# Layer norms with mean and reciprocal deviation in PSUM, and a last norm that works on two tiles an instruction

## The chip, the cores and the metric

One core of one Trainium2 chip runs the kernel. The metric is the device time of one execution in microseconds (us); of several runs the median counts. The profile is of one execution, and its times count from the first instruction.

## What is computed

The reference is a decoder trunk of two layers on 256 positions and 2048 features, in float32. Each layer has a mixer (RWKV-7 time mixing, then differential attention) and a gated MLP, and a layer norm behind each of the four:

```python
def layer_norm(x, g, b):
    xf = x.astype(jnp.float32)
    mu = xf.mean(-1, keepdims=True)
    var = jnp.square(xf - mu).mean(-1, keepdims=True)
    return ((xf - mu) * lax.rsqrt(var + LN_EPS) * g + b).astype(x.dtype)

for i in range(DEPTH):
    h = rwkv7_mix(...) if i % 2 == 0 else diff_attn_mix(...)
    x = layer_norm(ALPHA * x + h, ln_g[i, 0], ln_b[i, 0])
    x = layer_norm(ALPHA * x + conv_glu(x, ...), ln_g[i, 1], ln_b[i, 1])
```

## The kernel before

Features lie on the 128 partitions and positions along the free dimension, so the activations `X` are 16 tiles of 128 x 256. A planner decides where tiles lie, sets the waits and puts each engine's instructions in order from the data dependences and the order of the code; the order of an engine's queue in the profile need not be that of the code.

Nearly all of the time goes into products of weights with activations. A weight block arrives as float32 (`raw`), ScalarE rounds its high half (`hi`, L210), VectorE subtracts that to get the low half (`lo`, L213), and TensorE multiplies with both. Two column blocks of 128 make one `hi` and one `lo` of 128 x 256.

A norm has these steps. `ln_add` adds the mixer's product to `X` tile by tile; GpSimd keeps running sums of the tiles and of their squares (`ln_acc`, L370). `ln_stats` lets TensorE add the partitions up with a matrix of 1/2048 (L345): the mean lands in the first half of one PSUM bank (`lnst`), the mean square in the second. ScalarE squares the mean (L419) and copies it to SBUF as `ln_dm` (L420), VectorE makes the variance `ln_v` (L421), and `rsqrt` gives the reciprocal deviation `ln_rs`, in SBUF: logarithm and exponential on ScalarE (L319, L320), then one Newton step of three VectorE instructions (L321 to L323).

The norm is applied in two ways. Three norms are applied in the middle of the kernel while TensorE works ahead: `Ahead.run` multiplies the next six weight columns (L896 to L898) with activations that are scaled but not yet normed, takes `ln_stats` behind the fifth of thirty items, and lets `ln_apply` go on a tile at a time. There GpSimd subtracts the mean from each tile (L435), and the rest goes by the letter for the tile in `LEAD["r"]`: for twelve tiles VectorE multiplies by `ln_rs` (L444) and ScalarE applies scale and bias, both given as a column of 128 values (L445); for one tile VectorE does both (L452, L453); for three VectorE multiplies by scale and `ln_rs` in one instruction (L457). Then the tile is split into high and low halves (L191 on ScalarE, L192 on VectorE). The products made ahead are corrected in `total` (L304 to L307), which reads `ln_dm` and `ln_rs` too.

The last norm has nothing to run beside. `ln_finish` subtracts the mean (L472) on VectorE for the six tiles of `FIN_V` and on GpSimd for the other ten, multiplies by scale and `ln_rs` on VectorE (L480), adds the bias on ScalarE (L482), and SP stores two tiles at a time (L484).

Of the kernel before, what the change touches and what calls it, by code (L numbers as in the profile page):

```python
# [8 lines left out]
F32 = mybir.dt.float32  # L9
F32R = mybir.dt.float32r  # L10
AF = mybir.ActivationFunctionType
ALU = mybir.AluOpType
AX = mybir.AxisListType

P = 128
T = 256
D = 2048
KT = D // P
# [20 lines left out]
ORDER = [0, 1, 14, 2, 3, 4, 5, 6, 7, 15, 8, 9, 10, 11, 12, 13]  # L39
DBL = 64 * 16 + 16  # L40
LEAD = dict(q=9, p=(), e=1, a=1, s=4, n=0.301, d=8, h=0.1, r='ACAAAAAAAAAAABBB')
FIN_V = (0, 2, 5, 8, 11, 14)
FIN_S = range(2, KT + 1, 2)


def _param_layout():
# [79 lines left out]
class Trunk:  # L126
# [199 lines left out]
    def ln_begin(self, ahead=None, share=False):  # L326

        if self.ln_st is None:
            mk = lambda name, **k: self.ctx.enter_context(self.tc.tile_pool(name=name, bufs=1, side="right", **k))
            st = mk("lnst", space=bass.MemoryType.PSUM).tile([P, 2 * T], F32, name="lnst")  # L330
            self.ln_st = [st[:, :T], st[:, T:]]
            pool = mk("lnp")
            self.ln_dm, self.ln_rs, self.ln_c, self.ln_m2, self.ln_v = (
                pool.tile([P, T], F32, name=f"ln_{n}") for n in ("dm", "rs", "c", "m2", "v"))
            self.ln_sq = pool.tile([P, 4, T], F32, name="ln_sq")
            self.ln_acc = pool.tile([P, 2 * T], F32, name="ln_acc")
        self.ln_n, self.ln_open, self.ln_share, self.ln_first = 0, False, share, []
        self.ln_ahead, self.ln_last = ahead, []
        if ahead is not None:
            ahead.columns()  # L340
# [71 lines left out]
    def ln_stats(self):  # L412

        nc = self.nc
        sx, sq = self.ln_st
        self.ln_colsum((self.ln_acc[:, :T], self.ln_acc[:, T:]))
        for n, tiles in enumerate(self.ln_last):
            self.ln_colsum(tiles, n == len(self.ln_last) - 1)
        nc.scalar.activation(out=self.ln_m2, in_=sx, func=AF.Square)  # L419
        nc.scalar.copy(out=self.ln_dm, in_=sx)  # L420
        nc.vector.scalar_tensor_tensor(out=self.ln_v, in0=sq, scalar=LN_EPS, in1=self.ln_m2, op0=ALU.add,  # L421
                                       op1=ALU.subtract)
        self.rsqrt(self.ln_v, self.ln_rs, T, self.ln_m2)

    def ln_plain(self, i, h):
        self.ln_stats()
# [38 lines left out]

    def ln_finish(self, i, h, out):
        nc = self.nc
        at = 0

        def center(j):  # L470
            eng = nc.vector if j in FIN_V else nc.gpsimd
            eng.tensor_tensor(out=self.X[:, j, :], in0=self.X[:, j, :], in1=self.ln_dm, op=ALU.subtract)  # L472

        for j in range(-2, KT):
            if j < KT - 2:
                center(j + 2)
            if j < 0:
                continue
            x = self.X[:, j, :]
            nc.vector.scalar_tensor_tensor(out=x, in0=x, scalar=self.p(f"ln_g{i}{h}", j), in1=self.ln_rs, op0=ALU.mult,  # L480
                                           op1=ALU.mult)
            nc.scalar.activation(out=x, in_=x, func=AF.Identity, bias=self.p(f"ln_b{i}{h}", j))  # L482
            if j + 1 in FIN_S:
                nc.sync.dma_start(out=out[:, at:j + 1, :], in_=self.X[:, at:j + 1, :])  # L484
                at = j + 1

    def lead(self, feed, group, *args, ramp=0, ahead=4):

# [975 lines left out]
```

## Time and profile before

| | before |
|---|---|
| median of 3 runs | 2576.1 us (2573.64 to 2580.8) |
| the profiled execution | 2568.52 us |
| its span, first to last instruction | 2566.5 us |
| TensorE busy | 2468.5 us, 96% |
| VectorE busy | 2053.8 us, 80% |
| ScalarE busy | 1645.2 us, 64% |
| GpSimd busy | 390.7 us, 15% |
| mean granted TensorE clock | 0.981 |

PE is TensorE's matmul side and PEld its weight loads, DVE is VectorE, ACT is ScalarE, POOL is GpSimd and SP is SyncE, which issues the transfers. Durations of neighbours on one engine overlap a little, so the distance from start to start is what a queue costs. A granted clock of 1.00 is 2.4 GHz, one of 0.50 is 1.2 GHz.

### The profile page before, as it was taken

Reading aid. Unit: us, or ns where it says so; the run is one execution under the profiler, and the core shown is the slowest. Engines: PE = TensorE matmul, PEld = TensorE weight load, DVE = VectorE, ACT = ScalarE, POOL = GpSimd, SP = SyncE. Lnnn points to the kernel's source line nnn. Section 1 sums busy time; section 2 is a strip of 40 time slices with the busy share of each in tenths; the row PEclk is TensorE's granted clock in tenths of the full one; section 3 lists DMA queues with packets and bytes.
Section 4 is the critical chain, followed back from the end, with each engine's and each line's share of the span. In section 5 each row is a group of like instructions: output and inputs, shape, how many; then the busy total and the mean of one; then the engine's idle time right before and its main releaser. Section 6 shows DMA issues by size and latency. Waiting matters only on the chain.

```text
span 2566.5 us, 54810 instructions
## 1 busy us (share of the span) xinstructions
PE 2468.5 (96%) x17598; PEld 2171.5 (85%) x17598; DVE 2053.8 (80%) x5100; ACT 1645.2 (64%) x4318; POOL 390.7 (15%) x456
## 2 busy tenths in 40 slices
PE   7999989899899999999999999999999999999996
PEld 6888778767788888888889899998888888888886
DVE  8977888887897777777777877779997777777776
ACT  5765555644576666666566766666676666666664
POOL 4343344332400000000111200003300000000111
PEclk9999999999999999999999999999999999999998
DMA  6544334344466555556766555556465555566664
GB/s 191 175 129 116 102 104 108 99 121 124 125 187 192 190 190 190 190 189 184 225 190 183 156 171 171 171 167 196 145 199 188 188 188 188 188 186 185 189 190 127
DMA packets 285186, 429.63 MB, mean 167 GB/s; under 512 B 69081, under 2 KB 91617, under 8 KB 284897
## 3 DMA queue, kind: packets, MB, share of 16 engines
q1 hardware_dynamic: 284896, 426.14, 55.0%
q8 instruction: 137, 2.24, 0.4%
q14 instruction: 153, 1.25, 0.2%
HBM read 421.03 MB, written 6.57 MB: 167 GB/s over the span
## 4 chain that ended last, share of the span: by engine, by line
PE 74%; DVE 4%; ACT 1%; issue 1%; DMA 1%; POOL 0%; ACTq 0%; DVEq 0%; SPq 0%; POOLq 0%
PE psd L225 42%; PE psd L226 21%; PE psd L293 1%; PE psd L291 1%; PE psd L292 1%; DVE lo L213 1%; PE psd L897 1%; PE psd L896 1%; PE psd L898 1%; PE lnst L345 1%; PE psd L221 1%; PE psd L223 1%; PE psd L222 1%; DMA raw<-in_rw_o 0%; PE pss L656 0%
## 5 line engine op out<-in xcount | busy, mean ns | idle before, releaser
L210 ACT CAST hi<-raw 128x256 fp32r<-128x256 f32 (+1 forms) x3128 | 1231.1, 405 | 676.5 <-PE psd L225 461.2
L213 DVE TENSOR_TENSOR lo<-raw,hi 128x256 fp32r<-128x256 f32 (+1 forms) x2984 | 1287.5, 442 | 404.4 <-ACT hi L210 369.4
L225 PE MATMUL psd<-S,hi 128*128 128x512 f32 x3004 | 1056.7, 396 | 0.4 <-ACT hi L210 0.4
L226 PE MATMUL psd<-S,lo 128*128 128x256 f32 x3004 | 842.2, 280 | 4.4 <-DVE lo L213 3.8
L225 PEld LDWEIGHTS psd<-S,hi 128*128 128x128 f32 x3004 | 566.0, 188 | 132.5 <-ACT hi L210 1.2
L226 PEld LDWEIGHTS psd<-S,lo 128*128 128x128 f32 x3004 | 565.8, 188 | 5.9 <-DVE lo L213 4.5
L225 PE MATMUL psd<-hs,hi 128*128 128x512 f32 x1290 | 451.4, 394 | 0.1
L226 PE MATMUL psd<-hs,lo 128*128 128x256 f32 x1290 | 361.5, 280 | 0.0
L225 PEld LDWEIGHTS psd<-hs,hi 128*128 128x128 f32 x1290 | 241.8, 187 | 56.5 <-ACT hi L210 1.0
L226 PEld LDWEIGHTS psd<-hs,lo 128*128 128x128 f32 x1290 | 243.1, 188 | 0.4 <-DVE lo L213 0.3
L363 POOL COPY ln_acc<-X 128x256 f32<-128x256 f32 x4 | 2.1, 528 | 1230.9 <-DVE X L397 1230.9
L213 POOL TENSOR_TENSOR lo<-raw,hi 128x256 fp32r<-128x256 f32 x144 | 130.4, 913 | 301.2 <-ACT hi L210 244.1
L223 PE MATMUL psd<-S,lo 128*128 128x256 f32 x480 | 140.6, 293 | 13.8 <-DVE lo L213 8.4
L221 PE MATMUL psd<-S,hi 128*128 128x256 f32 x480 | 141.6, 295 | 0.9 <-ACT hi L210 0.5
L222 PE MATMUL psd<-S,hi 128*128 128x256 f32 x480 | 141.4, 295 | 0.0
L223 PEld LDWEIGHTS psd<-S,lo 128*128 128x128 f32 x480 | 92.8, 193 | 22.3 <-DVE lo L213 12.8
L225 PE MATMUL psd<-S1r,hi 128*128 128x512 f32 x276 | 109.9, 427 | 1.4 <-ACT o_rs L1049 0.7
L370 POOL TENSOR_TENSOR ln_acc<-ln_acc,X 128x256 f32<-128x256 f32 x49 | 40.9, 834 | 402.4 <-DVE X L409 389.1
L221 PEld LDWEIGHTS psd<-S,hi 128*128 128x128 f32 x480 | 92.5, 193 | 5.7 <-ACT hi L210 1.5
L222 PEld LDWEIGHTS psd<-S,hi 128*128 128x128 f32 x480 | 92.8, 193 | 2.9 <-issue 2.7
L221 PE MATMUL psd<-S1r,hi 128*128 128x256 f32 x284 | 87.2, 307 | 1.4 <-ACT S1r L191 0.9
L897 PE MATMUL psd<-S,lo 128*128 128x258 f32 x256 | 75.4, 295 | 10.1 <-DVE lo L213 10.1
(297 smaller groups left out, 3823.5 us busy)
## 6 DMA issues: line engine op xcount, KB each, us to landing
raw<-in_ff_up SPq DMA_DIRECT2D x676, 256.0 KB, 3.4
raw<-in_ff_down SPq DMA_DIRECT2D x320, 256.0 KB, 3.0
raw<-in_rkv SPq DMA_DIRECT2D x192, 256.0 KB, 3.5
raw<-in_da_qk SPq DMA_DIRECT2D x122, 256.0 KB, 3.4
raw<-in_da_v SPq DMA_DIRECT2D x64, 256.0 KB, 3.1
raw<-in_da_o SPq DMA_DIRECT2D x64, 256.0 KB, 3.5
raw<-in_rw_o SPq DMA_DIRECT2D x50, 256.0 KB, 3.5
raw<-in_ff_down SPq DMA_DIRECT2D x32, 192.0 KB, 2.7
```

The source lines that it names most:

```text
L210: nc.scalar.copy(out=hi[:, :s * P], in_=r)
L213: eng.tensor_tensor(out=lo[:, :s * P], in0=r, in1=hi[:, :s * P].bitcast(F32), op=ALU.subtract)
L221: nc.tensor.matmul(ps[:, :T], lhsT=hi, rhs=xs[:, :T], start=first, stop=False)
L222: nc.tensor.matmul(ps[:, :T], lhsT=hi, rhs=xs[:, T:], start=False, stop=False)
L223: nc.tensor.matmul(ps[:, :T], lhsT=lo, rhs=xs[:, :T], start=False, stop=last)
L225: nc.tensor.matmul(ps, lhsT=hi, rhs=xs, start=first, stop=False)
L226: nc.tensor.matmul(ps[:, T:], lhsT=lo, rhs=xs[:, :T], start=False, stop=last)
L291: nc.tensor.matmul(o, lhsT=xh, rhs=hi, start=k == 0 and b == 0, stop=False)
L292: nc.tensor.matmul(o, lhsT=xh, rhs=lo, start=False, stop=False)
L293: nc.tensor.matmul(o, lhsT=xl, rhs=hi, start=False, stop=k == KT - 1 and b == T // P - 1)
L370: nc.gpsimd.tensor_tensor(out=self.ln_acc[:, hs], in0=self.ln_acc[:, hs], in1=t, op=ALU.add)
L897: nc.tensor.matmul(ps[:, 2:4 + T], lhsT=lo[:, w], rhs=x[:, 2:4 + T], start=False, stop=False)
```

## The change

The two tiles `ln_mean` and `ln_rs` become names for the two halves of the PSUM bank `lnst`: the mean stays where TensorE wrote it, and the exponential writes the reciprocal deviation over the mean square. The SBUF tile `ln_rs` is gone; the copy `ln_dm` stays for GpSimd and for `total`. The three VectorE instructions of the Newton step are written anew, so that each has the deviation as an operand. `ln_apply` and `total` are not edited, but their `ln_rs` is now in PSUM.

`ln_finish` is new. Four pairs of tiles (those that start at 4, 6, 8 and 10) are centred on GpSimd, tile by tile, and four on VectorE, two tiles in one instruction of 512 columns whose second operand is the mean, given twice. Then VectorE multiplies two tiles at a time by `ln_rs`, ScalarE applies scale and bias together to each tile, and SP stores the pair.

```diff
-FIN_V = (0, 2, 5, 8, 11, 14)
-FIN_S = range(2, KT + 1, 2)
+FIN_P = (4, 6, 8, 10)
 ...
-            self.ln_dm, self.ln_rs, self.ln_c, self.ln_m2, self.ln_v = (
-                pool.tile([P, T], F32, name=f"ln_{n}") for n in ("dm", "rs", "c", "m2", "v"))
+            self.ln_dm, self.ln_c, self.ln_m2, self.ln_v = (
+                pool.tile([P, T], F32, name=f"ln_{n}") for n in ("dm", "c", "m2", "v"))
+
+            self.ln_mean, self.ln_rs = self.ln_st
 ...
-        self.rsqrt(self.ln_v, self.ln_rs, T, self.ln_m2)
+        l, rs = self.ln_m2, self.ln_rs
+        nc.scalar.activation(out=l, in_=self.ln_v, func=AF.Ln)
+        nc.scalar.activation(out=rs, in_=l, func=AF.Exp, scale=-0.5)
+        nc.vector.tensor_tensor(out=l, in0=self.ln_v, in1=rs, op=ALU.mult)
+        nc.vector.scalar_tensor_tensor(out=l, in0=l, scalar=-0.5, in1=rs, op0=ALU.mult, op1=ALU.mult)
+        nc.vector.scalar_tensor_tensor(out=rs, in0=l, scalar=1.5, in1=rs, op0=ALU.add, op1=ALU.mult)
 ...
     def ln_finish(self, i, h, out):
         nc = self.nc
-        at = 0
-
-        def center(j):
-            eng = nc.vector if j in FIN_V else nc.gpsimd
-            eng.tensor_tensor(out=self.X[:, j, :], in0=self.X[:, j, :], in1=self.ln_dm, op=ALU.subtract)
-
-        for j in range(-2, KT):
-            if j < KT - 2:
-                center(j + 2)
-            if j < 0:
-                continue
-            x = self.X[:, j, :]
-            nc.vector.scalar_tensor_tensor(out=x, in0=x, scalar=self.p(f"ln_g{i}{h}", j), in1=self.ln_rs, op0=ALU.mult,
-                                           op1=ALU.mult)
-            nc.scalar.activation(out=x, in_=x, func=AF.Identity, bias=self.p(f"ln_b{i}{h}", j))
-            if j + 1 in FIN_S:
-                nc.sync.dma_start(out=out[:, at:j + 1, :], in_=self.X[:, at:j + 1, :])
-                at = j + 1
+        wide = lambda t: t.unsqueeze(1).broadcast_to([P, 2, T])
+        for j in range(0, KT, 2):
+            xs = self.X[:, j:j + 2, :]
+            if j in FIN_P:
+                for k in range(2):
+                    nc.gpsimd.tensor_tensor(out=xs[:, k], in0=xs[:, k], in1=self.ln_dm, op=ALU.subtract)
+            else:
+                nc.vector.tensor_tensor(out=xs, in0=xs, in1=wide(self.ln_mean), op=ALU.subtract)
+        for j in range(0, KT, 2):
+            xs = self.X[:, j:j + 2, :]
+            nc.vector.tensor_tensor(out=xs, in0=xs, in1=wide(self.ln_rs), op=ALU.mult)
+            for k in range(2):
+                nc.scalar.activation(out=xs[:, k], in_=xs[:, k], func=AF.Identity, scale=self.p(f"ln_g{i}{h}", j + k),
+                                     bias=self.p(f"ln_b{i}{h}", j + k))
+            nc.sync.dma_start(out=out[:, j:j + 2, :], in_=xs)
```

## Rows read from the trace of the kernel before

**Rows 1.** The page: engines' totals, and the chain's shares by engine.

```profile
PE 2468.5 (96%) x17598; PEld 2171.5 (85%) x17598; DVE 2053.8 (80%) x5100; ACT 1645.2 (64%) x4318; POOL 390.7 (15%) x456
...
PE 74%; DVE 4%; ACT 1%; issue 1%; DMA 1%; POOL 0%; ACTq 0%; DVEq 0%; SPq 0%; POOLq 0%
```

**Rows 2.** Chain of waits in the tail: start, us, engine, tile and line.

```profile
2546.66 0.38 ACT ln_m L419
2547.05 0.27 ACT ln_dm L420
2547.34 0.42 DVE ln_v L421
...
2550.12 0.86 DVE ln_m L321
...
2555.29 0.87 DVE X L480
2556.19 6.10 ACT X L482 x15
```

**Rows 3.** Timeline of the tail: start, us, engine, line, operation; then idle before.

```profile
2547.39 8.48 POOL L472 TENSOR_TENSOR X<-X,ln_dm 128x256 f32<-128x256 f32 x10 [14.63 <-ACT ln_dm L420]
2547.68 2.44 DVE L472 TENSOR_TENSOR X<-X,ln_dm 128x256 f32<-128x256 f32 x3
...
2548.25 0.42 ACT L320 ACTIVATE ln_rs<-ln_m 128x256 f32<-128x256 f32 x1
...
2556.19 6.50 ACT L482 ACTIVATE X<-X,par 128x256 f32<-128x256 f32 x16 [7.52 <-DVE X L480]
```

**Rows 4.** Timeline of the first middle norm: GpSimd, VectorE and ScalarE.

```profile
692.12 13.74 POOL L435 TENSOR_TENSOR X<-X,ln_dm 128x256 f32<-128x256 f32 x16 [11.75 <-ACT ln_dm L420]
693.95 0.96 DVE L321 TENSOR_TENSOR ln_m<-ln_rs 128x256 f32<-128x256 f32 x1
694.97 0.41 ACT L210 CAST hi<-raw 128x256 fp32r<-128x256 f32 x1 [0.31 <-PE psd L898]
695.69 0.41 ACT L210 CAST hi<-raw 128x256 fp32r<-128x256 f32 x1 [0.31 <-PE psd L898]
...
699.24 0.95 DVE L444 TENSOR_TENSOR X<-X,ln_rs 128x256 f32<-128x256 f32 x1
700.22 0.60 ACT L445 ACTIVATE X<-X,par 128x256 f32<-128x256 f32 x1 [4.12 <-DVE X L444]
700.99 0.94 DVE L213 TENSOR_TENSOR lo<-raw,hi 128x256 fp32r<-128x256 f32 x1
...
703.46 0.94 DVE L213 TENSOR_TENSOR lo<-raw,hi 128x256 fp32r<-128x256 f32 x1
703.57 0.60 ACT L445 ACTIVATE X<-X,par 128x256 f32<-128x256 f32 x1 [0.16 <-DVE X L444]
704.08 0.39 ACT L210 CAST hi<-raw 128x256 fp32r<-128x256 f32 x1
...
706.07 0.41 DVE L213 TENSOR_TENSOR lo<-raw,hi 128x256 fp32r<-128x256 f32 x1
706.40 0.41 DVE L444 TENSOR_TENSOR X<-X,ln_rs 128x256 f32<-128x256 f32 x1
```

**Rows 5.** TensorE's waits, 699 to 712: us in total, times, longest.

```profile
PE psd L897 <- DVE lo L213: 3.7, 3, 1.5
```

**Rows 6.** Busy time by stretch: PE, PEld, DVE, ACT, POOL; clock, DMA share, GB/s.

```profile
703.00:705.00 2.00, 0.54 (x4) 0.54 (x5) 2.00 (x3) 1.84 (x6) 2.00 (x4) 1.00 0.39 125
...
707.00:709.00 2.00, 2.00 (x11) 2.00 (x11) 2.00 (x7) 2.00 (x6) 0.00 (x0) 0.50 0.27 85
```

**Rows 7.** Instructions of lines L403 and L409: count, ns minimum/median/maximum, first and last start.

```profile
L403 DVE SCALAR_TENSOR_TENSOR t<-X,ln_c x44: 411/955/970, 651.3 to 2531.2; 128x256 f32<-128x256 f32 x44
L409 DVE TENSOR_TENSOR X<-t,psd x56: 399/414/422, 656.1 to 2544.9; 128x256 f32<-128x256 f32 x56
```

**Rows 8.** Groups by form: busy us, mean ns, idle before.

```profile
L659 DVE SCALAR_TENSOR_TENSOR s<-pss,B 128x512 f32<-128x512 f32 x8 | 5.5, 688 | 0.0
```

## What was predicted

> **What bounds the kernel now.** I read the page's totals first. TensorE is busy 96% of the span, and three quarters of the chain that ended last is TensorE [rows 1]. So an edit on VectorE, ScalarE or GpSimd is worth something only where TensorE has finished or stands still. The change touches the four layer norms, and there are two such kinds of place.
>
> The first is the tail. The chain of waits in its last stretch [rows 2] leaves TensorE when the last column sum ends, at about 2546.6 us, and then runs through ScalarE and VectorE for 16 us: square and copy, the variance, six VectorE instructions that start 0.865 us apart (2550.12 to 2555.29), the first scaled tile, and sixteen bias activations. The last of these ends at 2562.69 (6.50 us from 2556.19, [rows 3]); what lies behind it (last store, landing, end at 2566.5) is 3.8 us.
>
> The second is the three middle norms, which run beside products. In the first of them the timeline [rows 4] shows GpSimd subtracting the mean from sixteen tiles for 13.74 us, 0.86 us each. For all that time VectorE's instructions take 0.95 us and start 0.87 us apart; when GpSimd is done they take 0.41 us and start 0.33 us apart (706.07, 706.40). One of VectorE's jobs here is the low half of each weight block ("lo"), and TensorE waits for it three times, 3.7 us together [rows 5]. In the table by stretches TensorE is busy 0.54 of 2 us at 703 to 705, and at 707 to 709 it is fully busy at a granted clock of 0.50, which is 1.2 GHz [rows 6]. The other two middle norms, near 1430 and near 1830 us, repeat this almost to the instruction, so the rows stand for one of three and what is found for one counts three times.
>
> **Why the operand's place matters.** Two rows from the same stretches, where GpSimd adds up the column sums, differ in one thing [rows 7]. L403 reads two SBUF tiles: median 955 ns, at best 411. L409 reads one SBUF and one PSUM tile: 414 ns, never above 422. So beside GpSimd a VectorE instruction with one operand in PSUM keeps its 0.41 us. The change gives just that to every instruction that uses the mean or the reciprocal deviation: the three steps of the reciprocal root (each now has the deviation as an operand), the scaling of every tile, and the last norm's centring.
>
> **The middle norms, step by step.** From 693.95 to 706 VectorE runs six such instructions under GpSimd's load: three root steps, and the scaling of tiles 0, 1 and 2. Each goes from 0.87 to about 0.34 us start to start, 3.2 us less. The lo blocks and the splits keep two SBUF operands and their 0.87 us while GpSimd runs. I let the queue run again with these lengths, in the same order. The lo block of 700.99 ends at 699.2; before, it ended at 701.93. The one of 703.46 ends at 701.2. The one of 706.07 starts at 702.9 and, now inside GpSimd's stretch, ends at 703.8 instead of 706.5. A lo block feeds TensorE for 0.72 us: the hi casts, released by TensorE, are that far apart (694.97, 695.69 in [rows 4]). ScalarE's queue stood behind the activation of tile 0 until 700.22 [rows 4]; it moves 2.1 us ahead with that tile, so the hi halves are there. Then TensorE finds the first two blocks in time and waits some 1.8 us for the third, which it starts at 703.85 instead of 706.53, 2.7 us earlier. The next two blocks come 0.4 us late each, because GpSimd still runs until about 705.3. That leaves 1.9 us; I take 1.8. What is late next is again a lo block, behind two splits of 0.87 us.
>
> After the stall TensorE ran at half clock from 706.5 to 709.9 and there did what takes 2 us at full clock, so 1.4 us were lost. Since some 2.6 us of standing still remain, I keep this loss in the forecast; if the clock stays up, a norm gives 3.3 us. Behind that TensorE is fully busy for tens of us, so what it gains carries to the end. Bounds for one norm: 0 (the waits are only moved) to 3.3 us. Three norms: 5.4 us, between 0 and 9.9.
>
> **The tail, step by step.** Up to the exponential, which ends at 2548.67 [rows 3], nothing changes. Before, VectorE filled its wait for it with three centrings (2547.68 on). Now the centrings read the mean from the PSUM bank into which the exponential writes. That different engines are kept apart in one bank shows in [rows 2]: the variance needs the square, which ended at 2547.04, but starts at 2547.34, when ScalarE's copy from the same bank has ended. So I put the centrings behind the exponential.
>
> The Trainium skill, "PSUM — Partial Sum Buffer", section "PSUM bank collisions raise a hardware error", says that two engines must never be in one bank and the same 32 partitions together, reads included, and that the compiler orders them. That speaks against this change. By the rule the tail is as summed below; without it two centrings would hide in front of the root, 1.2 us better. The trace agrees with the rule by the 0.30 us of the variance.
>
> From 2548.70 VectorE then has three root steps of 0.34 us (1.0), four centrings of two tiles, and the first scaling. A 512-column instruction that reads PSUM with a broadcast operand took 688 ns [rows 8]; less the 0.07 us by which neighbours overlap (0.41 against 0.34), that is 0.62 apart, so 2.5 us for the centrings and 0.69 for the scaling. All four stand ahead of the first scaling in the code, so I count all four: ScalarE starts at 2552.9. The order is the planner's; with pair 0 alone ahead it is 1.9 us better.
>
> Now the price of one activation with scale and bias. Bias alone: sixteen in 6.50 us of 0.50 each, so 0.40 start to start [rows 3]. With both as columns the activation takes 0.60 us, and the next starts 0.51 us behind it (703.57, 704.08 in [rows 4]). Sixteen cost 15 x 0.51 + 0.60 = 8.25 us where they cost 6.50. ScalarE so becomes the bound of the tail: VectorE's pairs come every 0.62 us and ScalarE needs 1.02 for one. It ends at 2561.1 instead of 2562.69: 1.6 us gained, though its first input comes 3.3 us earlier. GpSimd's eight centrings (0.73 to 0.90 us each) end by 2554.6 and the last of them is needed near 2557; they are covered by over 2 us. Eight stores were and are issued by SP, one for two tiles, the last behind the last activation: nothing.
>
> Not shown in the trace: ScalarE or VectorE writing such a tile into PSUM. For VectorE I bound it by 0.34 and 0.87 us per instruction (the two states of the same instruction in [rows 4]) and take the lower, as reads of PSUM show it. Two columns-fed activations in a row: between 0.40 and 0.60 start to start; I take 0.51, which is the same instruction before another one. So the tail lies between 4.5 us gained and nothing.
>
> **The sum.** 1.6 + 5.4 = 7.0 us. The profiled execution would go from 2568.5 to 2561.5. It was 7.6 us faster than the median of the runs; put on the median, 2576.1 - 7.0 = 2569.1 us.
>
> **Rivals.**
> Half clock goes too. If TensorE's shorter stalls leave the clock at 1.0, each norm gives 3.3 us: 1.6 + 9.9 = 11.5, so 2564.6. For it: two of the three waits vanish or nearly so. Against: 2.6 us of waiting remain of 3.7, most of them in one piece, and what followed 3.7 us may follow 2.6.
>
> The middle norms give nothing. The lo blocks still queue behind splits at 0.87 us, and GpSimd, ending only 0.5 us sooner, could keep TensorE's last wait where it is, or the planner could order VectorE's queue otherwise. Only the tail is left: 2574.5. For it: six short instructions among long ones; against: 3.2 us less work on a queue in which, by the rows, one instruction follows the other.
>
> Slower: the contention stays although one operand is in PSUM. Then the root steps cost 0.87 us and a two-tile centring 1.73 while GpSimd runs, until 2554.4. That holds three root steps and 1.8 centrings; 2.2 centrings and the scaling follow by 2556.5, and ScalarE ends 8.25 us later, at 2564.7: 2.0 us slower, with no gain in the middle, 2578.1. It decides at a first scaled pair later than 2554.4. Against it stand [rows 7].
>
> **How the numbers follow.** Forecast 0.50, with a range of its own from 2567 to 2572; clock stays up 0.25; middle gives nothing 0.18; contention stays 0.07. The range of 8 in 10 reaches to the second and third cases: 2563.5 to 2575.5. A measurement of this kernel tells 0.3%, 7.7 us, from no change. The forecast lies just inside it: I give a little under half of it (0.22) and all of the second case to faster, 0.47. Slower by as much needs the contention and lost order in the middle norms, 0.03; same is 0.50.
>
> **What would show it.** In the changed profile: the root steps and scalings near 0.41 us while GpSimd runs; TensorE's waits for lo about 2.6 instead of 3.7 us a norm; granted clock 0.5 behind each or not; in the tail, no centring before the exponential's end, ScalarE's first activation near 2552.9 less what was gained earlier, sixteen of them 0.51 apart. I am wrong if VectorE's order in the middle norms is another, or if those instructions still take 0.95 us.

## The result, and the profile after

Six runs of each kernel beside each other gave 2560.57 us after (2552.46 to 2566.5) against 2576.76 before (2571.47 to 2583.35), a ratio of 0.9934 with a 95% interval from 0.9910 to 0.9957. The forecast was 2569.1 with a range from 2563.5, so the kernel became faster by more than was forecast, and its time lies outside the range.

Where the time went is read from the start of each norm's square on ScalarE, which opens its statistics, because there the stages can be told apart. In microseconds:

| profiled execution | first square at | to the 2nd | to the 3rd | to the last | last square to span's end |
|---|---|---|---|---|---|
| before | 691.40 | 731.03 | 398.68 | 725.55 | 19.84 |
| after | 697.24 | 727.96 | 396.88 | 722.32 | 17.60 |
| gain | -5.8 | 3.1 | 1.8 | 3.2 | 2.2 |

Behind the first square 10.3 us are gained: 8.1 in the middle norms (forecast 5.4) and 2.2 in the tail (forecast 1.6). Ahead of it the changed kernel was 5.8 us later in this pair of profiles, although every engine runs the same instructions in the same order there. Over all the profiled executions of this study that first square stood between 687.5 and 703.5 us. So the medians contain a scatter of some microseconds that arises ahead of the changed instructions, and the distances between the squares are the better measure.

In the page's totals of after (busy us, share of the span, instructions), VectorE has 13 us less to do than in [rows 1], and the other engines are within a few us of what they were:

```profile
PE 2472.6 (97%) x17598; PEld 2172.2 (85%) x17598; DVE 2040.8 (80%) x5090; ACT 1645.8 (64%) x4318; POOL 388.1 (15%) x454
```

VectorE's and GpSimd's timeline in the first middle norm of after, which answers to [rows 4] (start, us, engine, line, operation):

```profile
697.92 0.42 DVE L422 SCALAR_TENSOR_TENSOR ln_v<-lnst,ln_m 128x256 f32<-128x256 f32 x1 [2.29 <-PE psd L901]
697.97 13.61 POOL L441 TENSOR_TENSOR X<-X,ln_dm 128x256 f32<-128x256 f32 x16 [12.26 <-ACT ln_dm L421]
...
699.79 0.41 DVE L427 TENSOR_TENSOR ln_m<-ln_v,lnst 128x256 f32<-128x256 f32 x1
700.13 0.63 DVE L212 TENSOR_TENSOR lo<-raw,hi 128x256 fp32r<-128x256 f32 x1
700.68 0.41 DVE L428 SCALAR_TENSOR_TENSOR ln_m<-ln_m,lnst 128x256 f32<-128x256 f32 x1
...
702.77 0.41 DVE L458 TENSOR_TENSOR X<-X,lnst 128x256 f32<-128x256 f32 x1
703.10 0.99 DVE L212 TENSOR_TENSOR lo<-raw,hi 128x256 fp32r<-128x256 f32 x1
704.01 0.82 DVE L459 TENSOR_SCALAR X<-X,par 128x256 f32<-128x256 f32 x1
704.75 0.96 DVE L212 TENSOR_TENSOR lo<-raw,hi 128x256 fp32r<-128x256 f32 x1
705.63 1.84 DVE L191 TENSOR_TENSOR S<-X,S 128x256 fp32r<-128x256 f32 x2
707.39 0.96 DVE L212 TENSOR_TENSOR lo<-raw,hi 128x256 fp32r<-128x256 f32 x1
708.28 0.41 DVE L450 TENSOR_TENSOR X<-X,lnst 128x256 f32<-128x256 f32 x1
```

Three things are to be seen. Every instruction with one operand in "lnst", the PSUM tile, takes 0.41 us while GpSimd is at work, as forecast. The lo block behind a root step costs 0.55 us start to start (700.13 to 700.68), where two operands in SBUF were counted at 0.87; but behind two such instructions in a row it costs 0.91 (703.10 to 704.01). And the scaling of tile 2, which stood at 702.59 in the kernel before, ahead of a lo block and both splits of tiles 0 and 1, now comes behind them (708.28).

TensorE's waits in the 13 us that answer to [rows 5], and the busy table (us of PE, PEld, DVE, ACT, POOL; granted clock, DMA share, GB/s) for the stretch of its longest wait, to set beside [rows 6]:

```profile
PE psd L900 <- DVE lo L212: 0.6, 2, 0.3
```

```profile
707.24:709.24 2.00, 1.67 (x14) 1.41 (x12) 2.00 (x5) 0.52 (x2) 2.00 (x3) 1.00 0.00 1
```

TensorE waits 0.6 us where it waited 3.7, its longest wait is 0.3 where it was 1.5, and the granted clock stays at 1.00 (2.4 GHz).

How much of this lasts is read from the same matmuls in both kernels. The busy table (columns as above) has the first 113 matmuls from the square on and the 118 behind them, first before, then after:

```profile
691.42:710.70 19.28, 15.54 (x113) 14.91 (x112) 18.43 (x31) 10.93 (x30) 13.74 (x16) 0.91 0.21 66
710.70:724.48 13.78, 13.78 (x118) 13.78 (x117) 13.07 (x39) 12.58 (x38) 0.64 (x1) 1.00 0.58 173
```

```profile
697.26:711.51 14.25, 13.92 (x113) 13.41 (x112) 13.41 (x23) 8.74 (x24) 13.54 (x16) 1.00 0.27 77
711.51:727.15 15.64, 15.18 (x118) 14.12 (x117) 14.86 (x44) 14.26 (x41) 0.06 (x1) 1.00 0.51 155
```

The first 113 take 5.0 us less than before, the next 118 take 1.9 us more. Of the 5.0 us that the change gains where GpSimd subtracts, 1.9 are given back behind it, while GpSimd has nothing to do (0.06 us) and VectorE is busy for 14.86 of 15.64 us.

The tail of after, by the timeline, beside [rows 2] and [rows 3]:

```profile
2544.40 0.38 ACT L420 ACTIVATE ln_m<-lnst 128x256 f32<-128x256 f32 x1 [0.80 <-PE lnst L346]
2545.12 5.52 POOL L479 TENSOR_TENSOR X<-X,ln_dm 128x256 f32<-128x256 f32 x8 [14.63 <-ACT ln_dm L421]
2545.98 0.39 ACT L426 ACTIVATE lnst<-ln_m 128x256 f32<-128x256 f32 x1
2546.40 0.42 DVE L427 TENSOR_TENSOR ln_m<-ln_v,lnst 128x256 f32<-128x256 f32 x1 [0.90 <-ACT lnst L426]
2546.86 0.42 DVE L428 SCALAR_TENSOR_TENSOR ln_m<-ln_m,lnst 128x256 f32<-128x256 f32 x1
2547.32 0.43 DVE L429 SCALAR_TENSOR_TENSOR lnst<-ln_m,lnst 128x256 f32<-128x256 f32 x1
2547.78 2.48 DVE L481 TENSOR_TENSOR X<-X,lnst 128x512 f32<-128x512 f32 x4
2550.18 4.86 DVE L484 TENSOR_TENSOR X<-X,lnst 128x512 f32<-128x512 f32 x8
2550.89 7.97 ACT L486 ACTIVATE X<-X,par 128x256 f32<-128x256 f32 x16 [4.52 <-DVE X L484]
```

VectorE stands idle until the exponential has ended, then does the root, all four centrings and only then the first scaling. ScalarE's sixteen activations follow at 0.49 us each and end at 2558.86, 14.46 us behind the square; before it was 16.03 (2546.66 to 2562.69).

### The profile page after: what moved, and what is told of

Read it like the earlier page. It is cut to its first block, busy times and chain, and to the rows that moved or that the text cites. A ratio compares the mean times of both kernels' runs of the same rounds, so it can differ in the third digit from the quotient of the medians.

```text
span 2562.0 us, 54782 instructions
## 1 busy us (share of the span) xinstructions
PE 2472.6 (97%) x17598; PEld 2172.2 (85%) x17598; DVE 2040.8 (80%) x5090; ACT 1645.8 (64%) x4318; POOL 388.1 (15%) x454
## 4 chain that ended last, share of the span: by engine, by line
PE 83%; DVE 10%; DMA 2%; issue 2%; ACT 2%; POOL 1%; SPq 0%; DVEq 0%; ACTq 0%; POOLq 0%
PE psd L224 42%; PE psd L225 22%; PE psd L220 3%; PE psd L222 3%; PE psd L221 3%; DVE lo L212 3%; PE psd L291 1%; PE psd L292 1%; PE psd L290 1%; DVE mx L776 1%; DVE S L191 1%; DMA raw<-in_rw_o 1%; PE pss L1145 1%; DVE S1r L191 1%; ACT hi L209 1%
## 5 line engine op out<-in xcount | busy, mean ns | idle before, releaser
L222 PE MATMUL psd<-S1r,lo 128*128 128x256 f32 x284 | 84.8, 299 | 1.5 <-DVE lo L212 1.4
```

Of the source, the lines that this page charges most:

```text
L222: nc.tensor.matmul(ps[:, :T], lhsT=lo, rhs=xs[:, :T], start=False, stop=last)
```

## The experiments

### Which place gives the time, and how sure it is

Four kernels were compared with the kernel before in one set of interleaved runs. Two are the kernels before and after, unchanged.

> The kernel before once more, to see how far one profile differs from another. Stages are measured by the start of the squaring of the mean (the first ScalarE instruction of a norm's statistics): 691.4, 1422.4, 1821.1 and 2546.7 us in the profile of before, 697.2, 1425.2, 1822.1 and 2544.4 in that of after. Theory A (the gain of the change lies only behind the first norm's statistics, about 10 us: 8.1 in the three distances between them, 2.2 in the tail; the rest of the measured 17 us is scatter of the first stage, whose queues are the same in both kernels): ratio 1.000, the three distances again 731.0, 398.7 and 725.6 within 1 us, the tail 19.8 from the last square to the end, and a first stage anywhere between 685 and 700. Theory B (the first stage too is shorter after the change, by some 7 us on the mean): the first stage within 2 us of 691.4 here, and in the kernels that carry the change some 7 us below.

> The changed kernel once more. Theory A (gain only behind the first statistics): ratio near 0.996 (10 us), distances 728.0, 396.9, 722.3 within 1 us, tail 17.6. Theory B (first stage too): ratio 0.9934 again, first stage below 688.

The third has the middle norms' part alone: the deviation in PSUM for every norm, and the last norm in its old form (from the kernel after):

```diff
-FIN_P = (4, 6, 8, 10)
+FIN_V = (0, 2, 5, 8, 11, 14)
...
-        wide = lambda t: t.unsqueeze(1).broadcast_to([P, 2, T])
...
+        def center(j):
+            eng = nc.vector if j in FIN_V else nc.gpsimd
+            eng.tensor_tensor(out=self.X[:, j, :], in0=self.X[:, j, :], in1=self.ln_dm, op=ALU.subtract)
...
+            nc.vector.scalar_tensor_tensor(out=x, in0=x, scalar=self.p(f"ln_g{i}{h}", j), in1=self.ln_rs, op0=ALU.mult,
+                                           op1=ALU.mult)
+            nc.scalar.activation(out=x, in_=x, func=AF.Identity, bias=self.p(f"ln_b{i}{h}", j))
```

> Mean and reciprocal deviation in PSUM as in the change, but the last norm written as before: single tiles, centred from the SBUF copy of the mean, scale and reciprocal deviation in one VectorE instruction, bias alone on ScalarE. Theory A: the three distances as after (728.0, 396.9, 722.3), gain 8 us there. In the tail, theory C (what counts there is that the root steps no longer wait for GpSimd): three root steps 0.35 instead of 0.87 us, so the first activation 1.6 us earlier than before and, with 0.40 us from one to the next, a tail of 18.2; ratio 0.996. Theory D (the pairs and the joint activation make the gain in the tail): tail 19.8 as before, ratio 0.997.

The fourth has the last norm's part alone: only there is the deviation in PSUM (from the kernel after):

```diff
-            self.ln_mean, self.ln_rs = self.ln_st
+            self.ln_mean, self.ln_rs = self.ln_st[0], self.ln_sb
...
+        if not wide:
+            return self.rsqrt(self.ln_v, self.ln_rs, T, self.ln_m2)
+        self.ln_rs = self.ln_st[1]
...
-                self.ln_stats()
+                self.ln_stats(True)
```

> The three middle norms as before, with the reciprocal deviation in SBUF; only the last norm has it in PSUM and is written as in the change. Theory A: distances 731.0, 398.7, 725.6 as before, tail 17.6, ratio 0.9991 (2.2 us). Theory B (first stage too, since the queues of that stage are those of the change): first stage some 7 us shorter, ratio 0.9965.

| kernel | median, us | ratio to before (95%) | distances of the squares | tail |
|---|---|---|---|---|
| before again | 2570.46 | 0.9999 (0.9986 to 1.0012) | 730.6, 398.9, 725.6 | 19.6 |
| after again | 2560.94 | 0.9966 (0.9953 to 0.9979) | 727.8, 397.0, 722.4 | 17.6 |
| middle norms alone | 2558.35 | 0.9963 (0.9949 to 0.9978) | 727.3, 396.8, 722.2 | 16.6 |
| last norm alone | 2568.79 | 0.9991 (0.9978 to 1.0004) | 730.6, 399.6, 725.7 | 17.6 |

The distances repeat to within 0.7 us in the first column and 0.2 in the last, and each part moves only its own columns. The middle column is less sure: a kernel below with the same middle norms has 398.2 there. The second comparison's ratio is worth 0.0034 x 2570.5 = 8.7 us, where the first's medians gave 16.2; the 10.3 us of the stages lie between. As a ratio they are 0.9960, inside the second interval and just outside the first. Theory A, by which the change is worth what happens behind the statistics, holds. Theory B, which looked for a part of the 16 us ahead of the first norm, falls as it was put: the changed kernel's first square stood at 693.3 here, not below 688. Over all profiles it stands at 687.5 to 697.2 with the changed middle norms and at 691.4 to 703.5 without; a small part there can't be told from scatter by single profiles.

What was not foreseen is the last row but one: with the old last norm, kept tile by tile, the tail is 16.6 us (18.2 by theory C, 19.8 by theory D), 1.0 less than with the new one. So in the tail all of the gain comes from the operands' place, and the rewritten form of the last norm takes 1.0 us of it away. VectorE's and ScalarE's timeline of that kernel:

```profile
2540.40 2.44 DVE L479 TENSOR_TENSOR X<-X,ln_dm 128x256 f32<-128x256 f32 x3
2542.76 0.41 DVE L428 TENSOR_TENSOR ln_m<-ln_v,lnst 128x256 f32<-128x256 f32 x1
2543.09 0.61 DVE L479 TENSOR_TENSOR X<-X,ln_dm 128x256 f32<-128x256 f32 x1
2543.63 0.41 DVE L429 SCALAR_TENSOR_TENSOR ln_m<-ln_m,lnst 128x256 f32<-128x256 f32 x1
...
2545.86 6.49 ACT L489 ACTIVATE X<-X,par 128x256 f32<-128x256 f32 x16 [4.51 <-DVE X L487]
```

The centrings here read the mean's copy in SBUF (ln_dm), and three of them are done while ScalarE works on the logarithm and the exponential. The others cost 0.54 us start to start between root steps (2543.09 to 2543.63), and root step and centring together 0.87, where the kernel before paid 0.865 for each [rows 2]; theory C had counted only the root steps as shorter.

But the filled wait is not what makes this tail shorter than the new one. ScalarE's first activation starts 6.48 us behind the square (2539.38 to 2545.86), in after 6.49 (2544.40 to 2550.89). The difference is ScalarE's: sixteen activations with bias alone take 6.49 us, sixteen with scale and bias 7.97. Of these 1.5 us the end behind the last activation, 3.6 us here and 3.1 in after, gives 0.5 back.

### Root steps, scalings or their order

Four kernels tell the parts of the middle norms apart. Each was executed once beside the kernel before, so only the distances are compared. In the first (from after) the exponential writes to SBUF and only the last root step writes to PSUM, so the root steps have two SBUF operands and the scalings one:

```diff
-        nc.scalar.activation(out=rs, in_=l, func=AF.Exp, scale=-0.5)
-        nc.vector.tensor_tensor(out=l, in0=self.ln_v, in1=rs, op=ALU.mult)
+        nc.scalar.activation(out=e, in_=l, func=AF.Exp, scale=-0.5)
+        nc.vector.tensor_tensor(out=l, in0=self.ln_v, in1=e, op=ALU.mult)
...
```

> The three root steps work in SBUF as before; only the last of them writes the reciprocal deviation into PSUM, where the scalings read it. VectorE's order in the middle norms is that of the changed kernel (tile 2 is scaled behind the splits of tiles 0 and 1). Theory P (the place of the operand makes the gain, in each instruction beside GpSimd and in the lo block behind it): root steps and the lo blocks between them again 0.87 us from start to start, so tile 0 is scaled as late as before; the scalings 0.34 us; about half of the gain, 1 to 2 us in the first and third distance (729.5 and 724 us), TensorE's waits behind the first statistics about 2 us. Theory O (the new order makes it): distances as after the change, 728.0 and 722.3.

The second is its mirror: the same lines, with e in PSUM and the finished rs in SBUF:

```diff
-            self.ln_mean, self.ln_rs = self.ln_st
+            self.ln_mean, self.ln_e = self.ln_st
...
```

> The opposite half: the root steps read their operand from PSUM, the last writes the reciprocal deviation to SBUF, and the scalings read it there. VectorE's order in the middle norms is that of the kernel before (tile 2 is scaled ahead of a lo block and both splits). Theory P (place of the operand): root step and lo block together 0.88 us where they took 1.76, so tile 0 is scaled 2.6 us sooner behind the square than before; scalings 0.87 us; some 1.5 to 2.5 us of the 3.1 us in the first distance, waits of 1.5 to 2 us. Theory O (order): distances as before, 731.0 and 725.6, waits 3.7 us.

The third is the kernel before without GpSimd's sixteen subtractions in each middle norm:

```diff
...
-            if j < KT - 2:
-                center(j + 2)
```

> The kernel before without GpSimd's sixteen subtractions of the mean in each of the three middle norms, which are left out, not moved; all operands in SBUF, VectorE's order as before. Theory P, in its form that GpSimd's reads are what lengthens VectorE's two-SBUF instructions: every one of them takes 0.41 us, TensorE waits for lo less than 0.5 us, the granted clock stays at 1.00, and the distances are those of the change or a little less, 727.5 and 722. If something else than GpSimd lengthens them: 0.95 us, waits of 3.7 us and distances as before.

The fourth is the kernel before with the scalings issued in the order that the kernel after has:

```diff
-                nc.vector.tensor_tensor(out=x, in0=x, in1=self.ln_rs, op=ALU.mult)
+                if j > 1:
+                    with self.tc.issue_after(second.ins):
+                        nc.vector.tensor_tensor(out=x, in0=x, in1=self.ln_rs, op=ALU.mult)
...
```

> The kernel before, all operands in SBUF, with the scaling of tile 2 and of the later tiles held behind the split of tile 1 on VectorE's queue, which gives the changed kernel's order up to there. Theory P (place of the operand): the two lo blocks that came behind tile 2's scaling come one 0.87 us slot sooner, nothing else; waits 2.5 to 3 us instead of 3.7, gain at most 1 us a norm. Theory O (order): distances as after, 728.0 and 722.3.

| kernel | 1st distance (gain) | last distance (gain) | TensorE's waits behind the 1st statistics, longest |
|---|---|---|---|
| before | 731.03 | 725.55 | 3.7, 1.5 |
| roots in SBUF, scalings in PSUM | 729.01 (2.0) | 724.07 (1.5) | 2.2, 1.6 |
| roots in PSUM, scalings in SBUF | 730.11 (0.9) | 724.34 (1.2) | 2.7, 1.6 |
| both in PSUM (after) | 727.96 (3.1) | 722.32 (3.2) | 0.7, 0.3 |
| order alone | 730.66 (0.4) | 725.53 (0.0) | 2.8, 1.2 |
| no subtractions on GpSimd | 724.68 (6.4) | 719.31 (6.2) | none |

The places give the time and the order next to none, so theory P holds and theory O falls. The two places add up: 2.0 + 0.9 is 2.9 of 3.1 in the first norm and 1.5 + 1.2 is 2.7 of 3.2 in the last. The kernel with its roots in SBUF and the one with the order alone came out as P had them; the one with its scalings in SBUF gained less and waited longer than P had it. VectorE's rows of the first two kernels show what a place is worth. First roots in SBUF, then roots in PSUM:

```profile
699.12 0.95 DVE L428 SCALAR_TENSOR_TENSOR ln_m<-ln_m,ln_e 128x256 f32<-128x256 f32 x1
700.00 0.96 DVE L212 TENSOR_TENSOR lo<-raw,hi 128x256 fp32r<-128x256 f32 x1
700.88 0.96 DVE L429 SCALAR_TENSOR_TENSOR lnst<-ln_m,ln_e 128x256 f32<-128x256 f32 x1
```

```profile
690.93 0.41 DVE L428 SCALAR_TENSOR_TENSOR ln_m<-ln_m,lnst 128x256 f32<-128x256 f32 x1
691.26 0.63 DVE L212 TENSOR_TENSOR lo<-raw,hi 128x256 fp32r<-128x256 f32 x1
691.81 0.41 DVE L429 SCALAR_TENSOR_TENSOR ln_rs<-ln_m,lnst 128x256 f32<-128x256 f32 x1
```

A root step and its lo block cost 1.76 us in the first (699.12 to 700.88) and 0.88 in the second (690.93 to 691.81). That the pair costs 0.88, what one instruction with two SBUF operands cost before, is no accident. GpSimd's subtractions in after, one by one:

```profile
700.43 0.93 POOL L441 TENSOR_TENSOR X<-X,ln_dm 128x256 f32<-128x256 f32 x1
701.31 0.92 POOL L441 TENSOR_TENSOR X<-X,ln_dm 128x256 f32<-128x256 f32 x1
702.20 0.91 POOL L441 TENSOR_TENSOR X<-X,ln_dm 128x256 f32<-128x256 f32 x1
703.07 0.73 POOL L441 TENSOR_TENSOR X<-X,ln_dm 128x256 f32<-128x256 f32 x1
```

They start 0.88 us apart, and so do the lo blocks of after (700.13, 701.01, 701.89): the two engines take turns, one subtraction for one VectorE instruction with two SBUF operands. The instruction with a PSUM operand needs no turn and runs during GpSimd's, so it costs nothing beside the lo block, and a root step in PSUM saves a whole turn of 0.88 us. Two in a row last too long for that. Behind the two scalings at 702.44 and 702.77 the lo block starts together with GpSimd's next subtraction (703.10 and 703.07); the lo block has its full 0.91 us, and this subtraction takes 0.73.

The run without subtractions went past both theories: 6 us a norm, twice what the change gives. In it every VectorE instruction behind the statistics takes 0.41 to 0.43 us, and TensorE waits for nothing in the 40 us that follow. So what the change left is due to the subtractions too, but only in part to their traffic at the time. Of the 3.3 us between that kernel and after in the first norm, 1.1 have come about when 110 matmuls have started (13.17 us behind the square without subtractions, 14.25 in after); the rest comes behind GpSimd's last subtraction, in the second row of the busy table of after. There VectorE runs 44 instructions, 14.86 us of 15.64, which reads as work that is left over from GpSimd's stretch. Leaving the subtractions out also frees the scalings from having to follow a subtracted tile; the two were not told apart.

### Can VectorE take the subtractions itself?

If GpSimd's traffic were all that is left, VectorE could subtract the mean from its PSUM copy at 0.33 us a tile. All sixteen tiles were moved there, and, in another kernel, six of sixteen. Two further kernels ask what the last norm's order is worth. All four were compared with the kernel before in one set of interleaved runs.

The new last norm, pair by pair instead of all centrings first, with scale and bias of three tiles on VectorE (from after):

```diff
+FIN_O = (0, 2, 4, 6, 12, 8, 14, 10)
+FIN_V = (9, 15, 11)
...
+        for j in FIN_O:
             xs = self.X[:, j:j + 2, :]
+            if j not in FIN_P:
                 nc.vector.tensor_tensor(out=xs, in0=xs, in1=wide(self.ln_mean), op=ALU.subtract)
             nc.vector.tensor_tensor(out=xs, in0=xs, in1=wide(self.ln_rs), op=ALU.mult)
...
```

> The kernel after with the last norm put in another order: pairs are centred and scaled in turn, in the order of tiles 0, 2, 4, 6, 12, 8, 14, 10, GpSimd's four pairs are issued first, and VectorE does scale and bias of tiles 9, 15 and 11 itself. Theory C (the tail is paced by when the first scaled pair is there and then by ScalarE's 0.49 us an activation): with one centring of 0.61 ahead of the first scaling instead of four, ScalarE starts some 1.9 us sooner, and with thirteen activations instead of sixteen it ends another 1 us sooner, so that last square to span's end goes from 17.6 to about 14.8 us. Theory D (the end is set by the stores or by GpSimd's centrings): 16.5 to 17.6. Middle norms as after by both (first distance 728, last 722.3). Ratio 0.995 to 0.997.

The old last norm with three centrings on VectorE instead of six, to fit them into its wait for the exponential (from the kernel with the middle norms alone):

```diff
-FIN_V = (0, 2, 5, 8, 11, 14)
+FIN_V = (0, 1, 8)
```

> The middle norms of the kernel after; the last norm tile by tile as before, with reciprocal deviation in PSUM, and VectorE centring three tiles (0, 1 and 8) instead of six, GpSimd thirteen. By the earlier run with six, the tail was 16.6 us, and one centring stood between two root steps at 0.61 us. Theory C: with all of VectorE's centrings in its wait for the exponential the root is uninterrupted and VectorE's three late centrings (0.6 us each) go from its path: 15.6 us. Theory D (GpSimd's thirteen centrings, 0.73 to 0.86 us each, some 10.5 us from 0.1 us behind the variance, become late): 16.6 or more. Middle norms as after by both. Ratio 0.995 to 0.997.

All sixteen subtractions of the middle norms on VectorE (from after):

```diff
-            nc.gpsimd.tensor_tensor(out=self.X[:, j, :], in0=self.X[:, j, :], in1=self.ln_dm, op=ALU.subtract)
+            nc.vector.tensor_tensor(out=self.X[:, j, :], in0=self.X[:, j, :], in1=self.ln_mean, op=ALU.subtract)
```

> The kernel after with the sixteen subtractions of the mean in each middle norm moved from GpSimd to VectorE, which reads the mean from PSUM; GpSimd has nothing to do there. Leaving these subtractions out of the kernel before gave distances between the norms' squares of 724.7 and 719.3 (first and last). Theory G (what is left to gain in the middle norms is what GpSimd's traffic costs VectorE, and VectorE has room): sixteen more instructions of 0.34 us are 5.4 us of VectorE, the blocks and splits go from 0.87 to 0.34; distances 725.5 to 727.5 and 720 to 722, waits of TensorE under 1.5 us, better than the kernel after by 0.5 to 2 us a norm. Theory V (VectorE's queue itself is the bound behind the statistics): the 5.4 us come on top of 724.7 and 719.3, distances 729 to 730 and 723.5 to 725, slower than after by 1 to 2 us a norm.

Six of the sixteen (from the kernel with three centrings):

```diff
+MID_V = (3, 6, 9, 11, 13, 15)
...
+            if j in MID_V:
+                nc.vector.tensor_tensor(out=self.X[:, j, :], in0=self.X[:, j, :], in1=self.ln_mean, op=ALU.subtract)
```

> As the kernel with three of the last norm's centrings on VectorE, and in each middle norm VectorE centres six of the sixteen tiles (3, 6, 9, 11, 13, 15) from the mean in PSUM, GpSimd the other ten. GpSimd's stretch there should be 8.6 us instead of 13.6. Theory G: the blocks and splits behind 8.6 us fall to 0.34 apart, for six more instructions of 0.34 (2 us); distances 726.5 to 727.5 and 721 to 722, 0.5 to 1.3 us better than after. Theory V: 728.5 or more and 723 or more, no better than after. Tail as in that kernel, about 15.6. Ratio 0.994 to 0.996 by G.

| kernel | median, us | ratio to before (95%) | distances of the squares | tail |
|---|---|---|---|---|
| pair by pair | 2556.64 | 0.9936 (0.9919 to 0.9953) | 728.1, 397.3, 722.1 | 16.0 |
| three centrings | 2562.21 | 0.9954 (0.9937 to 0.9971) | 727.8, 398.2, 722.5 | 15.5 |
| all sixteen on VectorE | 2571.21 | 0.9999 (0.9985 to 1.0014) | 731.1, 400.3, 727.2 | 17.6 |
| six of sixteen, three centrings | 2559.38 | 0.9950 (0.9932 to 0.9967) | 726.5, 397.4, 723.9 | 15.5 |

With all sixteen on VectorE the contention is gone and so is the whole gain of the middle norms, as theory V of a full VectorE queue had it, and by more. The busy table of that kernel says where it went, and then its waits:

```profile
717.83:719.83 2.00, 2.00 (x19) 2.00 (x18) 2.00 (x7) 1.76 (x5) 0.00 (x0) 1.00 0.83 258
...
721.83:723.83 2.00, 0.00 (x0) 0.00 (x0) 2.00 (x7) 2.00 (x8) 0.00 (x0) 1.00 0.00 0
723.83:725.83 2.00, 0.00 (x0) 0.00 (x0) 1.83 (x5) 1.87 (x9) 0.85 (x1) 1.00 0.00 0
...
727.83:729.83 2.00, 2.00 (x8) 1.71 (x7) 2.00 (x7) 0.41 (x1) 0.68 (x1) 0.50 0.81 232
```

```profile
PE psd L225 <- DVE lo L212: 5.1, 1, 5.1
```

TensorE runs at full rate until 719.8. Then VectorE is behind, and TensorE waits 5.1 us in one piece, after which the granted clock is 0.50 (1.2 GHz). Six of sixteen on VectorE gives 1.4 us in the first norm, as theory G had it, and takes 1.6 in the last, as theory V had it: no better than the kernel after in sum.

The tails went as theory C had it where centrings leave the path (15.5 against a forecast of 15.6). Pair by pair gave 16.0 where 14.8 was expected: ScalarE started 1.7 us sooner, near the 1.9 expected, and ended at 11.97 us behind the square, but 4.0 us lie between that and the end of the span, where after has 3.1. Its last store is issued 0.24 us behind the last activation and takes 2.7 us to land, in after 2.0.

All but the one with all sixteen beat the kernel before. Three centrings and pair by pair are 2.1 and 1.6 us better than after in the tail; over all stages behind the first square that leaves 0.9 and 1.3 us. That is under 0.1% of the whole. The medians can't order these kernels: the first two are 5.6 us apart, as are the first squares of their profiled executions (691.31 and 696.89), while the sums of their columns differ by 0.4 us.

## Why the prediction was wrong, step by step

**Where the time is lost: right.** Each part moved only the stretches behind the statistics and the tail. That the three middle norms repeat one another "almost to the instruction" is right for the stall: in the second norm too it has three waits of 1.2, 1.5 and 1.1 us before and two of 0.3 and 0.2 after. It is not right for what follows: the second gave 1.8 us and the others 3.1 and 3.2. In the 40 us behind its square TensorE's waits fell only from 5.1 to 3.2 us, and 2.4 of these are no part of the stall:

```profile
PE pss L899 <- ACT hi L209: 1.0, 1, 1.0
PE psd L291 <- DVE lo L212: 1.0, 1, 1.0
PE psd L900 <- DVE lo L212: 0.6, 2, 0.3
PE psd L290 <- DVE lw L928: 0.4, 1, 0.4
PE pss L900 <- DVE lo L212: 0.2, 1, 0.2
```

**"What it gains carries to the end": wrong.** The prediction read from the kernel before that TensorE is fully busy for tens of us behind the stall, and took this over for the kernel after. In the first norm 1.9 us of 5.0 are given back in the next 118 matmuls, where TensorE was busy for all of 13.78 us before and is for 15.18 of 15.64 after; in the second the two waits of 1.0 us are such a loss.

**A PSUM operand frees the instruction: right.** 0.41 us beside GpSimd, for the root steps and for the scalings. The two lines of [rows 7] differ in the operation too, not in one thing alone; the runs with one half of the operands moved leave the place as the cause.

**The middle norms' term: mis-sized, 5.4 forecast, 8.1 measured.** The step that failed is "the lo blocks and the splits keep two SBUF operands and their 0.87 us while GpSimd runs". A lo block takes turns with GpSimd, and a root step with a PSUM operand fits into GpSimd's turn, so the lo block behind it costs 0.55. Run again with that number, the queue gives what the chip did. The lo block forecast to start 10.8 us behind the variance (692.08 to 702.9) started 9.47 behind it (697.92 to 707.39). Of these 1.35 us, 1.0 are three lo blocks at 0.33 less, and 0.34 the scaling that the planner moved behind it. So "in the same order" failed as well, but the order alone is worth next to nothing by its own run; what it is worth with the operands in PSUM was not run.

**"I keep this loss in the forecast": wrong.** It rested on 2.6 us of standing still, most in one piece. What remained was 0.6 us with 0.3 as its longest, and the clock stayed at 1.00. The rival that has the clock stay up, 11.5 us in sum, came nearest to the 10.3 of the stages; I gave it half the chance of the forecast. That its 3.3 us a norm lie near the 2.7 measured is in part luck: the stall gave 5.0 us, and what was given back behind it is in no case of the prediction.

**The tail's term: right in its mechanism and nearly in its size, 1.6 forecast, 2.2 measured.** Up to the last activation it is 1.57 (16.03 to 14.46). Inside that two errors cancel: three root steps that depend on one another are 0.46 apart (2546.40, 2546.86, 2547.32), not 0.34, which made ScalarE 0.25 late, and sixteen activations took 7.97 us, not 8.25. The other 0.7 us is the end behind the last activation, 3.8 us before and 3.1 after, which I had at the same length ("nothing" for the stores). It is the way of the last store from its issue to its landing (KB, us), before and after:

```profile
out_y<-X SPq DMA_DIRECT2D x1, 256.0 KB, 2.7
```

```profile
out_y<-X SPq DMA_DIRECT2D x1, 256.0 KB, 2.0
```

Before, the last stores are issued 0.8 us apart, after 1.0; with the old form of the last norm, which has them 0.8 apart again, the last one takes 2.5 us. No run changes the stores alone, so that their distance is the cause is not shown.

The centrings did stand behind the exponential, and all four did stand ahead of the first scaling. The reason given for the first, that the exponential writes to the bank that they read, is not needed: with the roots in SBUF the exponential does not touch the bank, and the centrings stand behind the whole root all the same, while VectorE is idle for 0.93 us:

```profile
2547.98 0.42 DVE L427 TENSOR_TENSOR ln_m<-ln_v,ln_e 128x256 f32<-128x256 f32 x1 [0.93 <-ACT ln_e L426]
...
2550.17 2.48 DVE L481 TENSOR_TENSOR X<-X,lnst 128x512 f32<-128x512 f32 x4
```

There it is their place in VectorE's queue; for after itself the two were not told apart, so the order came out as forecast and its reason is not shown. What the rewritten form costs against the old one, 1.0 us, is not this order but ScalarE's activation, 0.49 us apart with scale and bias where bias alone has 0.40. The prediction had that price (1.75 us for sixteen) but never set the change against the new operands in the old form.

**The contention that stays although one operand is in PSUM: excluded** by every row with lnst.

**The range: a term was left out.** It was made from the terms of the sum alone. The median of the kernel before itself was 2576.76, 2570.46 and 2573.08 us in the three comparisons, and the first square scatters over 16 us among profiles. A gain of 10.3 us was therefore measured as 16.2 once and 8.7 once. With the 6.3 us by which the kernel before moved (2576.76 to 2570.46) put below the rival's 2564.6, the range would have reached to 2558.3 and held the time. What the scatter ahead of the first norm comes from stays open; the second and third comparison did not run on the same chip.

## What to carry to other kernels

Where VectorE works beside GpSimd, count turns and not instructions: here one VectorE instruction with two SBUF operands went with each GpSimd subtraction, 0.88 us the pair, and one with a PSUM operand fitted in between for nothing. A wait of TensorE can cost twice, as the wait and as time at half clock behind it: give the second a term of its own. Follow a gain past the stall where it is made, because the queue that caused the stall can take some of it back (here 1.9 of 5.0 us). Moving work from a contending engine onto the engine that it slows can cost as much as the contention did; ask first whether that engine has room until the work is due.

## What the runs showed of the hardware that was not expected

- VectorE beside GpSimd: instructions with two SBUF operands and GpSimd's subtractions alternate, one for one, 0.88 us the pair (after, 700.13 to 702.20). Alone such a VectorE instruction is 0.34 us from the next (706.07, 706.40 in [rows 4]). One with a PSUM operand takes 0.41 us in GpSimd's stretch too. GpSimd's sixteen subtractions went from 13.74 to 13.61 us only. The Trainium skill, "SBUF — State Buffer", section "Who interferes with whom", says that a VectorE instruction with two SBUF inputs contends with a GpSimd instruction that reads SBUF, and one with at most one, outside the 2-port perf modes, does not. The traces agree with both halves (0.95 and 0.41); the price and the turns are from the rows alone. One instruction with a single SBUF operand is slower beside GpSimd, TENSOR_SCALAR X<-X,par: 0.82 us (704.01 in after), 0.41 without subtractions. Whether it ran in such a mode no row shows.
- Dependent VectorE instructions of 256 columns are 0.46 us apart in the tail of after (2546.40, 2546.86), a root step and an independent lo block behind it 0.34 (699.79, 700.13).
- ScalarE's exponential took 0.39 us into PSUM (2545.98 in after) and 0.42 into SBUF [rows 3].
- The granted clock fell to 0.50 behind three waits with 1.5 us as the longest [rows 5, 6] and behind one of 5.1 us, and stayed at 1.00 behind two with 0.3 as the longest. It also stayed at 1.00 behind one wait of 2.2 us (six of sixteen, first norm) and behind three with 1.6 as the longest (roots in PSUM, scalings in SBUF, second norm), so the longest wait alone does not tell.
